# Bias rows written once and read back overlapping, and high parts before low parts within a granule, in a two-layer encoder on one Trainium2 core

## The chip, the cores and the metric

The kernel runs on one core of one Trainium2 chip. The metric is device microseconds for one execution of the whole program, the median of several runs. Times inside a profile are microseconds from the start of the profiled span, unless marked ns.

## The reference, cut to what matters

Input x is 256 tokens by 2048 features, float32. The trunk has two layers. Layer 0: RMSNorm, differential attention with a shared relative-position bias, residual, RMSNorm, squared-ReLU MLP (2048 to 8192 to 2048), residual. Then keys, values and forget gates are computed once from the stream. Layer 1: RMSNorm, queries, forgetting attention over these keys and values, residual, a second MLP, residual, final RMSNorm. The bias, which the change touches, is added to every score of layer 0:

```python
rel = key_pos[None, :] - q_pos[:, None]
bias = jnp.transpose(rel_table[t5_bucket(rel)], (2, 0, 1)).astype(f32)
mask = (key_pos[None, :] // CHUNK) <= (q_pos[:, None] // CHUNK)
s = jnp.where(mask, s + bias[None, :, None], NEG)
```

The bias of a head depends only on key position minus query position, so for each of the 8 heads a row of 383 numbers holds all that is needed.

## The kernel before, in words

Every large product is float32 by three products of shorter numbers: a weight granule is split into a high part (`whi`, a cast on ACT, L180) and a low part (`wlo`, a subtraction on DVE, L183), and the activations are split the same way into the two halves of a 512-column tile, high in columns 0 to 255, low in 256 to 511. High times high, high times low and low times high are added up in PSUM.

A granule is 512 KB of weights. It is loaded into one of four `raw` buffers by SP's queue (`load`, L172), split into one of five `whi` and five `wlo` buffers, and used by one step of PE. A load into a raw buffer waits until the low part of the granule four before has been taken. The main loop (L984) goes through the steps of `order`; at step s it emits the functions registered in `pre[s]`, the split of the granules up to four ahead (three before step 8), `mid[s]`, the low parts and the next loads, the matmuls of the step, and `post[s]`. Instructions of one engine run in that order.

There are two kinds of unit. In a token-major unit ("B", `mm_b`, L185) the activations are the stationary operand: a granule is two blocks of 128 rows by 512 columns, and each needs three matmuls of 512 columns for each of two token halves (L194 to L196), 12 matmuls a step. In a feature-major unit ("A", `mm_a`, L198) the weights are stationary: a granule is four blocks of 128 rows by 256 columns. For each block j and each half n of its columns there is one matmul with the high part over all 512 columns of the activations (`whole`, L209) and one with the low part over the first 256 (`part`, L212), so 8 pairs a step and 4 steps a unit. They alternate, except at k = 15, where `part` comes first. Queries, keys and the MLP's first product are feature-major units.

The bias is prepared early. In `post[5]`, PE multiplies the table by a one-hot matrix (`bias_rows`, L338); the matrix `oh` is an input that the host makes in `bucket_onehot` (L1020). In `pre[6]`, after ACT's sums of squares (`stats0`), `bias_out` copies the 8 rows of 383 numbers to SBUF with DVE (L342) and writes them by SP's queue to a DRAM tile F, each row 128 times (L344). In `pre[8]`, after the evacuation of the first unit and the split of the gate weights (`split_wf`, L967), `bias_in` reads T from F by SP's queue (L352): partition q gets of each head the 256 numbers that begin at 127 - q of the row, by stepping through F with a row length one shorter than it is. POOL then sets the masked quarter of T to a large negative number (L353). The softmax (L414, L415) adds a slice of T to the scores on DVE.

Of the kernel before, what the change touches and what calls it, by code (L numbers as in the profile page):

```python
# [11 lines left out]
F32 = mybir.dt.float32  # L12
# [8 lines left out]
P = 128  # L21
D = 2048
S = 256
HD = 128
FF = 8192
NA = 8
# [3 lines left out]
NEG = -1e30  # L30
# [4 lines left out]
NREL = 383  # L35
# [7 lines left out]
def kernel(ctx: ExitStack, tc: tile.TileContext, *args):  # L43
    (x, rel_table, attn_g, mlp_g, w_qkv, lq1, lk1, lq2, lk2, subln_g, w_o_a, kv_g,
     w_k, w_v, w_f, b_f, w_q, w_o_b, w_in, w_out, fin_g, onehot, out) = args
    nc = tc.nc
# [5 lines left out]
    dr = ctx.enter_context(tc.tile_pool(name="dr", bufs=1, space=DRAM))  # L52
# [29 lines left out]
    h = [sb.tile([P, 2, CW], F32, tag=f"h{c}", name=f"h{c}") for c in range(NCH)]  # L82
# [115 lines left out]
    def mm_a(u, g, k0):  # L198
        bank, xs = u.bank, u.xs()
        hi = g.hi.rearrange("p (k c) -> p k c", k=g.kk)  # L200
        lo = g.lo.rearrange("p (k c) -> p k c", k=g.kk)
        for j in range(g.kk):
            k = k0 + j
            xt = xs[k // 2][:, k % 2, :]
            for n in range(2):
                w = slice(n * P, (n + 1) * P)

                def whole():
                    nc.tensor.matmul(bank[n], hi[:, j, w], xt, start=k == 0, stop=k == 15)  # L209

                def part():
                    nc.tensor.matmul(bank[n][:, 0:S], lo[:, j, w], xt[:, 0:S], start=False, stop=False)  # L212

                if k == 15:
                    part()
                    whole()
                else:
                    whole()
                    part()


    def new_x(tag):
# [111 lines left out]
    bias = {}  # L334
# [5 lines left out]
    def bias_out():  # L340
        bs = sb.tile([NA, 512], F32, tag="e", bufs=2, name="bs")
        nc.vector.tensor_copy(out=bs[:, 0:NREL], in_=bias["p"][0:NA, 0:NREL])  # L342
        F = dr.tile([NA, P, NREL], F32, tag="F", name="F")
        nc.sync.dma_start(out=F, in_=bs[:, 0:NREL].unsqueeze(1).broadcast_to([NA, P, NREL]))  # L344
        bias["F"] = F

    def bias_in():
        T = sb.tile([P, NA, S], F32, tag="tnc", bufs=2, name="T")

        src = bias["F"].rearrange("h q r -> h (q r)")[:, 127:127 + P * (NREL - 1)]  # L350
        src = src.rearrange("h (q r) -> q h r", r=NREL - 1)[:, :, 0:S]
        nc.sync.dma_start(out=T, in_=src)  # L352
        nc.gpsimd.memset(T[0:64, :, 192:256], NEG)  # L353
        bias["T"] = T

    def build_lambda():
# [38 lines left out]
    def diff_head(hd):  # L395
# [13 lines left out]
        def softmax(qt):  # L409
            def run():  # L410
                nk = P * (qt + 1)
                sc = st["sc", qt]
                s = sb.tile([P, 2, S], F32, tag="ssb", bufs=2, name="ssb")
                b = bias["T"][:, hd, S - nk:S].unsqueeze(1).broadcast_to([P, 2, nk])  # L414
                nc.vector.scalar_tensor_tensor(out=s[:, :, 0:nk], in0=sc[:, :, 0:nk], scalar=SCALE, in1=b,  # L415
                                               op0=ALU.mult, op1=ALU.add)
                nm = sb.tile([P, 2], F32, tag="nm", bufs=2, name="nm")
                nc.vector.tensor_reduce(out=nm, in_=s[:, :, 0:nk], op=ALU.max, axis=AX.X, negate=True)
                e = sb.tile([P, 2, S], F32, tag="e", bufs=2, name="e")
                rs = sb.tile([P, 2], F32, tag="rsum", bufs=2, name="rsum")  # L420
                for c in range(2):
                    nc.scalar.activation(out=e[:, c, 0:nk], in_=s[:, c, 0:nk], func=AF.Exp,
                                         bias=nm[:, c:c + 1], accum_out=rs[:, c:c + 1])
                st["e", qt] = e, rs
            return run
# [497 lines left out]
    n, ng = len(order), len(grs)  # L923
# [25 lines left out]
    g = grs[0]  # L949
    split_tiles(g)  # L950
    for k in range(2):
        w = slice(k * CW, (k + 1) * CW)
# [24 lines left out]
    n0.plan(7, lag=2)  # L977
    post[5].append(bias_rows)
    pre[6].append(bias_out)
    pre[8].append(bias_in)  # L980
    pre[12].append(build_lambda)

    ns = LA - 1
    for s in range(n + 2):  # L984
# [13 lines left out]
        if s < n:  # L998
            u, i, ms = order[s]
            if u.bank is None:  # L1000
                if u.apart:
                    u.bank = [ps.tile([P, 512], F32, tag="sc", name="sc") for _ in range(2)]
                else:
                    u.acc = ps.tile([P, 2, 512], F32, tag="acc", name="acc")
                    u.bank = [u.acc[:, m, :] for m in range(2)]
                if u.start is not None:
                    u.start(s)
            g = u.gs[i]
            if u.kind == "B":
                mm_b(u, g, 2 * i, ms)  # L1010
            else:
                mm_a(u, g, 4 * i)
            if i == len(u.gs) - 1:
                u.done(u, s, ms)
# [4 lines left out]

def bucket_onehot():  # L1020

    rel = np.arange(-255, NREL - 255)
    n = np.abs(rel)
    large = 8 + sum((n >= t).astype(np.int64) for t in (12, 16, 23, 32, 46, 64, 91))
    b = np.where(rel > 0, 16, 0) + np.where(n < 8, n, large)
    return (np.arange(32)[:, None] == b[None, :]).astype(np.float32)
# [25 lines left out]
```

## Time and profile before

| | us |
|---|---|
| median of three runs | 2245.37 |
| lowest and highest of the three | 2244.74, 2245.7 |
| the profiled execution | 2244.49 |
| its span in the profile | 2242.7 |

Busy time of an engine is the time in which it ran instructions. Issues of DMAs and waits are not counted as busy. Matmuls are pipelined: the end of one is modelled and overlaps the start of the next, so the pace of PE is read from the distance of starts. PEld is PE's loading of stationary operands, which overlaps its matmuls. The chain of work that ended last is followed back from the last instruction to what released it. In rows, `acc<-x,whi` reads: tile acc is written from tiles x and whi. The granted clock is given as a share of full speed, 1.00 being 2.4 GHz and 0.50 being 1.2 GHz. "SPq" is SP's DMA queue; a row of it covers the issue and, where several issues are merged, the time between them.

### The profile page before, as it was taken

The page shows a single profiled execution, that of the slowest core. Times are in us where ns is not written, and L with a number is a line of the kernel's source. Part 1 is how long each engine was busy: PE and PEld are TensorE (multiplying, and loading weights), DVE is VectorE, ACT ScalarE, POOL GpSimd, SP SyncE. Part 2 cuts the span into 40 slices and gives each one's busy share as a digit, 9 for nine tenths or more (in the row PEclk, how much of TensorE's full clock was granted, in tenths as well). Part 3 has the DMA queues.
Part 4 walks back from the last instruction along what each step waited for, and adds up shares of the span by engine and source line. Part 5 has one row for each costly group of instructions (what it writes and reads, how often), then busy time and mean ns, then how long its engine had stood idle before and what let it go on. Part 6 is the DMA issues. An engine that isn't in the chain of part 4 may idle for free.

```text
span 2242.7 us, 28986 instructions
## 1 busy us (share of the span) xinstructions
PE 2213.4 (99%) x11272; PEld 1877.7 (84%) x11272; DVE 1356.7 (60%) x1768; ACT 1020.8 (46%) x1343; POOL 13.6 (1%) x19
## 2 busy tenths in 40 slices
PE   8799999999999999999999999999999999999998
PEld 6688888888888888888888888888888888888886
DVE  4566666665565566566576566656655655655655
ACT  4455545544344344344554444454434444444443
POOL 0000000000000000000001000000000000000000
PEclk9899999999999999999999999999999999999999
DMA  7665555556656656655556565556566566566564
GB/s 199 199 183 172 166 170 183 173 188 201 183 185 202 195 180 195 192 187 189 177 170 204 173 194 186 180 170 201 183 200 189 185 193 186 188 197 180 187 202 135
DMA packets 319332, 416.06 MB, mean 186 GB/s; under 512 B 15066, under 2 KB 218972, under 8 KB 319068
## 3 DMA queue, kind: packets, MB, share of 16 engines
q1 hardware_dynamic: 319148, 414.20, 58.9%
q8 instruction: 88, 1.44, 0.3%
q14 instruction: 48, 0.39, 0.1%
q10 hardware_dynamic: 48, 0.02, 0.0%
HBM read 410.49 MB, written 3.68 MB: 185 GB/s over the span
## 4 chain that ended last, share of the span: by engine, by line
PE 97%; DMA 2%; DVE 0%; ACT 0%; issue 0%; SPq 0%; DVEq 0%; ACTq 0%
PE acc L209 32%; PE acc L212 16%; PE acc L194 15%; PE acc L196 15%; PE acc L195 15%; DMA raw<-in_w_qkv_a 2%; PE tp L232 1%; PE sc L405 0%; PE sc L748 0%; PE sc L194 0%; PE sc L195 0%; PE sc L196 0%; PE o L806 0%; DMA h<-in_x 0%; PE fp L619 0%; PE o L807 0%
## 5 line engine op out<-in xcount | busy, mean ns | idle before, releaser
L183 DVE TENSOR_TENSOR wlo<-raw,whi 128x1024 fp32r<-128x1024 f32 x767 | 926.1, 1225 | 627.4 <-ACT whi L180 626.8
L180 ACT CAST whi<-raw 128x1024 fp32r<-128x1024 f32 x767 | 795.9, 1048 | 730.5 <-PE acc L196 443.5
L209 PE MATMUL acc<-x,whi 128*128 128x512 f32 x2816 | 996.1, 399 | 17.5 <-ACT whi L180 17.5
L212 PE MATMUL acc<-x,wlo 128*128 128x256 f32 x2816 | 777.7, 281 | 0.5 <-DVE wlo L183 0.5
L209 PEld LDWEIGHTS acc<-x,whi 128*128 128x128 f32 x2816 | 525.7, 188 | 139.6 <-ACT whi L180 17.8
L212 PEld LDWEIGHTS acc<-x,wlo 128*128 128x128 f32 x2816 | 532.9, 189 | 9.2 <-DVE wlo L183 1.0
L194 PE MATMUL acc<-whi,hx 128*128 128x512 f32 x1120 | 436.9, 390 | 0.0
L196 PE MATMUL acc<-whi,hx 128*128 128x512 f32 x1120 | 436.0, 389 | 0.0
L195 PE MATMUL acc<-wlo,hx 128*128 128x512 f32 x1120 | 435.8, 389 | 0.0
L196 PEld LDWEIGHTS acc<-whi,hx 128*128 128x128 f32 x1120 | 210.2, 188 | 43.8
L195 PEld LDWEIGHTS acc<-wlo,hx 128*128 128x128 f32 x1120 | 210.3, 188 | 43.5
L194 PEld LDWEIGHTS acc<-whi,hx 128*128 128x128 f32 x1120 | 210.3, 188 | 43.1
L316 DVE TENSOR_TENSOR zs<-acc,z 128x512 f32<-128x512 f32 x96 | 66.3, 691 | 103.8 <-ACT z L315 103.8
L315 ACT COPY z<-acc 128x512 f32<-128x512 f32 x96 | 56.3, 587 | 157.9 <-PE acc L209 157.9
L590 ACT CAST hx<-s 128x512 fp32r<-128x512 f32 x64 | 39.7, 620 | 143.3 <-DVE s L588 143.3
L194 PE MATMUL acc<-whi,x 128*128 128x512 f32 x256 | 103.4, 404 | 0.0
L195 PE MATMUL acc<-wlo,x 128*128 128x512 f32 x256 | 100.5, 393 | 0.0
L196 PE MATMUL acc<-whi,x 128*128 128x512 f32 x256 | 100.5, 392 | 0.0
L209 PE MATMUL acc<-hx,whi 128*128 128x512 f32 x256 | 91.6, 398 | 0.0
L591 DVE TENSOR_TENSOR hx<-s,hx 128x512 fp32r<-128x512 f32 x64 | 44.3, 692 | 43.9 <-ACT hx L590 43.9
L212 PE MATMUL acc<-hx,wlo 128*128 128x256 f32 x256 | 70.5, 281 | 0.0
L327 DVE TENSOR_TENSOR h<-acc,h 128x512 f32<-128x512 f32 x88 | 56.7, 686 | 14.9 <-PE acc L196 14.9
(172 smaller groups left out, 1169.8 us busy)
## 6 DMA issues: line engine op xcount, KB each, us to landing
raw<-in_w_mlp_in SPq DMA_DIRECT2D x256, 512.0 KB, 4.0
raw<-in_w_mlp_out SPq DMA_DIRECT2D x256, 512.0 KB, 4.2
raw<-in_w_qkv_a SPq DMA_DIRECT2D x96, 512.0 KB, 4.5
raw<-in_w_o_a SPq DMA_DIRECT2D x32, 512.0 KB, 4.3
raw<-in_w_v_b SPq DMA_DIRECT2D x32, 512.0 KB, 3.8
raw<-in_w_k_b SPq DMA_DIRECT2D x32, 512.0 KB, 3.9
raw<-in_w_q_b SPq DMA_DIRECT2D x32, 512.0 KB, 4.2
raw<-in_w_o_b SPq DMA_DIRECT2D x32, 512.0 KB, 3.7
```

What stands on the lines that cost most here:

```text
L180: nc.scalar.copy(out=g.hi, in_=g.raw)
L183: nc.vector.tensor_tensor(out=g.lo, in0=g.raw, in1=g.hi, op=ALU.subtract)
L194: nc.tensor.matmul(bank[m], xh, hi[:, j, :], start=k == 0, stop=False)
L195: nc.tensor.matmul(bank[m], xh, lo[:, j, :], start=False, stop=False)
L196: nc.tensor.matmul(bank[m], xl, hi[:, j, :], start=False, stop=k == nk - 1)
L209: nc.tensor.matmul(bank[n], hi[:, j, w], xt, start=k == 0, stop=k == 15)
L212: nc.tensor.matmul(bank[n][:, 0:S], lo[:, j, w], xt[:, 0:S], start=False, stop=False)
L315: nc.scalar.copy(out=z1, in_=u.acc[:, :, S:2 * S])
L316: nc.vector.tensor_tensor(out=zs, in0=u.acc[:, :, 0:S], in1=z1, op=ALU.add)
L327: nc.vector.tensor_tensor(out=h[c][:, m, :], in0=u.bank[m], in1=h[c][:, m, :], op=ALU.add)
L590: nc.scalar.copy(out=t[:, :, 0:S], in_=s)
L591: nc.vector.tensor_tensor(out=t[:, :, S:2 * S], in0=s, in1=t[:, :, 0:S], op=ALU.subtract)
```

## The change

The host's one-hot matrix is made for relative positions 127 down to -255 instead of -255 up to 127, so that the rows come out reversed. F holds each row once (8 x 383) and is written by ACT's queue. T is read by ACT's queue with a source that overlaps itself: partition q reads, of each head, the 256 numbers that begin at q of the row, so T is reversed along the keys. The mask's memset moves to the first 64 columns and the softmax reads the first nk numbers of T backwards. Apart from this, `mm_a` takes all eight matmuls with the high parts of a granule in a row, then the eight with the low parts; the special order at k = 15 goes.

```diff
-        for j in range(g.kk):
-            k = k0 + j
-            xt = xs[k // 2][:, k % 2, :]
-            for n in range(2):
-                w = slice(n * P, (n + 1) * P)
...
-                if k == 15:
-                    part()
-                    whole()
-                else:
-                    whole()
-                    part()
+        tiles = [(j, n, xs[(k0 + j) // 2][:, (k0 + j) % 2, :], slice(n * P, (n + 1) * P))
+                 for j in range(g.kk) for n in range(2)]
+        for j, n, xt, w in tiles:
+            nc.tensor.matmul(bank[n], hi[:, j, w], xt, start=k0 + j == 0, stop=False)
+        for j, n, xt, w in tiles:
+            nc.tensor.matmul(bank[n][:, 0:S], lo[:, j, w], xt[:, 0:S], start=False, stop=k0 + j == 15)
...
-        F = dr.tile([NA, P, NREL], F32, tag="F", name="F")
-        nc.sync.dma_start(out=F, in_=bs[:, 0:NREL].unsqueeze(1).broadcast_to([NA, P, NREL]))
+        F = dr.tile([NA, NREL], F32, tag="F", name="F")
+        nc.scalar.dma_start(out=F, in_=bs[:, 0:NREL])
...
-        src = bias["F"].rearrange("h q r -> h (q r)")[:, 127:127 + P * (NREL - 1)]
-        src = src.rearrange("h (q r) -> q h r", r=NREL - 1)[:, :, 0:S]
-        nc.sync.dma_start(out=T, in_=src)
-        nc.gpsimd.memset(T[0:64, :, 192:256], NEG)
+        F = bias["F"]
+        src = bass.AP(F.tensor, F.offset, [[1, P], [NREL, NA], [1, S]])
+        nc.scalar.dma_start(out=T, in_=src)
+        nc.gpsimd.memset(T[0:64, :, 0:64], NEG)
...
-                b = bias["T"][:, hd, S - nk:S].unsqueeze(1).broadcast_to([P, 2, nk])
+                b = bias["T"][:, hd, 0:nk][:, ::-1].unsqueeze(1).broadcast_to([P, 2, nk])
...
-    rel = np.arange(-255, NREL - 255)
+    rel = np.arange(127, 127 - NREL, -1)
```

## Rows read from the trace of the kernel before

**Rows 1.** The page: busy time, and the chain's shares by engine.

```profile
PE 2213.4 (99%) x11272; PEld 1877.7 (84%) x11272; DVE 1356.7 (60%) x1768; ACT 1020.8 (46%) x1343; POOL 13.6 (1%) x19
...
PE 97%; DMA 2%; DVE 0%; ACT 0%; issue 0%; SPq 0%; DVEq 0%; ACTq 0%
```

**Rows 2.** The page, groups by line: busy us, mean ns, idle before.

```profile
L209 PE MATMUL acc<-x,whi 128*128 128x512 f32 x2816 | 996.1, 399 | 17.5 <-ACT whi L180 17.5
L212 PEld LDWEIGHTS acc<-x,wlo 128*128 128x128 f32 x2816 | 532.9, 189 | 9.2 <-DVE wlo L183 1.0
L209 PE MATMUL acc<-hx,whi 128*128 128x512 f32 x256 | 91.6, 398 | 0.0
```

**Rows 3.** The chain in order of time, 25 to 80: start, us, what.

```profile
33.25 1.04 ACT whi L180
...
35.57 30.16 DMA raw<-in_w_qkv_a
```

**Rows 4.** Timeline of SP's DMA queue, 25 to 66: start, us, issue.

```profile
29.44 0.82 SPq L344 DMA_DIRECT2D F<-bs  x1
35.57 13.97 SPq L172 DMA_DIRECT2D raw<-in_w_qkv_a  x2
64.38 0.37 SPq L352 DMA_DIRECT2D T<-F  x1
```

**Rows 5.** Windows of 5 us: busy PE, PEld, DVE, ACT, POOL, clock, DMA share, GB/s.

```profile
55.00:60.00 5.00, 0.00 (x0) 0.00 (x0) 0.00 (x0) 0.00 (x0) 0.00 (x0) 0.50 0.47 50
...
65.00:70.00 5.00, 2.62 (x7) 1.93 (x8) 2.69 (x3) 2.09 (x2) 0.16 (x1) 0.50 0.97 317
```

**Rows 6.** Timeline of PE before, around and after the stall: start, us, instruction.

```profile
34.62 0.50 PE L209 MATMUL acc<-x,whi 128*128 128x512 f32 x1
...
49.13 0.28 PE L212 MATMUL acc<-x,wlo 128*128 128x256 f32 x1
66.91 0.80 PE L209 MATMUL acc<-x,whi 128*128 128x512 f32 x1 [17.50 <-ACT whi L180]
...
72.29 0.39 PE L209 MATMUL acc<-x,whi 128*128 128x512 f32 x1
```

**Rows 7.** DMA issues: count, KB each, median us to landing.

```profile
raw<-in_w_qkv_a SPq DMA_DIRECT2D x96, 512.0 KB, 4.5
...
gf<-in_final_norm_g SPq DMA_DIRECT2D x1, 1024.0 KB, 7.0
...
C<-fg_nc SPq DMA_DIRECT2D x1, 16.0 KB, 4.7
```

**Rows 8.** ACT's timeline; T's users: ns min/median/max, first and last start.

```profile
38.71 0.41 ACT L967 CAST wfs<-wf_raw 128x256 fp32r<-128x256 f32 x1
...
L415 DVE SCALAR_TENSOR_TENSOR ssb<-sc,T x16: 415/554/685, 86.2 to 334.8; 128x256 f32<-128x256 f32 x8, 128x512 f32<-128x512 f32 x8
```

**Rows 9.** Timeline of PE within a feature-major unit, around 500 us.

```profile
500.02 0.28 PE L212 MATMUL acc<-x,wlo 128*128 128x256 f32 x1
...
501.08 0.28 PE L212 MATMUL acc<-x,wlo 128*128 128x256 f32 x1
```

**Rows 10.** The same within a token-major unit: a matmul, and its twelfth successor.

```profile
333.60 0.39 PE L194 MATMUL acc<-whi,hx 128*128 128x512 f32 x1
...
336.32 0.39 PE L194 MATMUL acc<-whi,hx 128*128 128x512 f32 x1
```

**Rows 11.** The same at the end of a feature-major unit, 77 to 79.

```profile
77.47 0.40 PE L212 MATMUL acc<-x,wlo 128*128 128x256 f32 x2
77.71 0.40 PE L209 MATMUL acc<-x,whi 128*128 128x512 f32 x1
...
78.07 0.62 PE L209 MATMUL acc<-x,whi 128*128 128x512 f32 x2
78.52 0.28 PE L212 MATMUL acc<-x,wlo 128*128 128x256 f32 x1
```

**Rows 12.** The chain in order of time, 374 to 376: eight transposes.

```profile
374.71 0.87 PE tp L232 x8
```

More of the change, by code (lines that the diff above doesn't have):

```diff
@@ L201, in mm_a @@
         lo = g.lo.rearrange("p (k c) -> p k c", k=g.kk)
-        for j in range(g.kk):
-            k = k0 + j
-            xt = xs[k // 2][:, k % 2, :]
-            for n in range(2):
-                w = slice(n * P, (n + 1) * P)
[L208 to L212, printed above, removed]
-                if k == 15:
-                    part()
-                    whole()
-                else:
-                    whole()
-                    part()
+        tiles = [(j, n, xs[(k0 + j) // 2][:, (k0 + j) % 2, :], slice(n * P, (n + 1) * P))
[4 more added lines that the diff above has]
+            nc.tensor.matmul(bank[n][:, 0:S], lo[:, j, w], xt[:, 0:S], start=False, stop=k0 + j == 15)
     def new_x(tag):
```

## The prediction

> **What bounds the kernel now.** I began with the page's share of busy time and its chain. PE is busy for 2213.4 of 2242.7 us, and the chain that ended last lies 97% on PE and 2% on a DMA [rows 1]. So a step counts only if it shortens what PE does, or a stretch in which PE stands. The groups by line show both: the first matmul line of the feature-major units holds 17.5 us of idle time, put down to ACT's high parts, and these units issue 2816 + 256 = 3072 such matmuls, each with a partner of 256 columns from the low parts [rows 2]. With eight pairs to a granule that is 384 granules.
>
> Next, the stall. The chain in order of time shows one piece of 30.16 us on a raw load that starts at 35.57, and the high part that PE waits for comes after its end [rows 3]. The DMA queue's timeline shows what stood before it: the write of F at 29.44, then two raw loads within 13.97 us, then nothing until the read of T at 64.38 [rows 4]. The windows show why the load crawls: at 55 to 60 us the DMA engines are 0.47 busy but move 50 GB/s, at a granted clock of 0.50; once F is through, 317 GB/s are moved [rows 5]. F is 8 x 128 rows of 383 words, out of eight partitions, 1.5 MB; it keeps about half of the engines occupied at a low rate, and the raw loads share them.
>
> **The change, part by part.**
>
> *The write of F.* It shrinks from 1024 rows of 1532 bytes to 8 of them and moves from SP's queue to ACT's. What goes is the stall. PE's last low part before it starts at 49.13, and 0.12 us later the next matmul would have started, at 49.25. PE starts again at 66.91 at half clock, 1.2 GHz after 2.4 GHz, and has done seven pairs by 72.29 [rows 6]. Seven pairs at the regular pace (0.3533 us, below) take 2.47 us. So the stall with its slow restart costs 72.29 - 49.25 - 2.47 = **20.6 us**. Nothing hides it, since PE is the chain before and after. The low end is 17.5 us, the idle time alone [rows 2]; more than 20.6 can't come out, since PE has no other idle time of this size.
>
> Is something else late instead? The load of 35.57 (the granule at which PE stopped) would land after about 4.5 us, the median of its kind [rows 7], at 40, nine us ahead of 49.25. SP no longer stands at the read of T, so later loads follow each freed buffer. What is new is on ACT. The issue of F stands behind ACT's squares and ahead of the cast at 33.25 [rows 3]; SP's issue of it took 0.82 us [rows 4]. At 4.7 us to landing, as the 16 KB write of C took [rows 7], it lands near 38. ACT comes to the issue of T after the cast of the gate weights, 38.71 to 39.1 [rows 8], so that wait comes out at about nothing. Behind it on ACT stand the high parts of the granules three and four ahead of PE; PE, which began its feature-major granules at 34.62 [rows 6] and takes 2.83 us for each, reaches the first of them after 43, so some 3 us of lateness are covered. T still moves 1 MB. Repeated reads of few bytes have a near row, the final gain's 1 MB in 7.0 us [rows 7], so T lands near 46; it is first used at 86.2 [rows 8], which becomes 65.6. The SBUF end has 128 partitions as before. While T moves, raw loads share the engines, but these moved 317 GB/s beside the same T read [rows 5] and PE needs 512 KB per 2.83 us, 185 GB/s. Cost: nothing, at most 5 us if T's megabyte comes ahead of a load at the rate of that 7.0 us row.
>
> *Reversal.* The one-hot table comes reversed from the host, the DVE add in the softmax reads its bias with step -1, the mask's memset moves to the first 64 columns. DVE is 60% busy [rows 1] and hidden by PE; 16 adds of 0.42 to 0.69 us [rows 8] could double without being seen. Cost nothing.
>
> *The order of matmuls.* The count stays; only neighbours change. Regular pairs: the low part at 500.02 is followed by its third successor at 501.08, so three pairs take 1.06 us, 0.3533 each, a granule 2.827 [rows 9]. In token-major units, where 512 columns follow 512 columns, twelve take 336.32 - 333.60 = 2.72 us, **0.2267** each [rows 10]. So of a pair's 0.3533, 0.1267 are left for the low part, while half of 0.2267 is 0.1133. The difference could belong to the low part (the next weights not ready under so short a matmul), or to the change of size. At a unit's end the code already puts two low parts and two high parts next to each other, and there two low parts take 77.71 - 77.47 = 0.24, **0.12** each, and two high parts 78.52 - 78.07 = 0.45, 0.225 each [rows 11]. Runs of eight short matmuls with weights of their own go at 0.87 / 8 = 0.109 us in the transposes [rows 12], so weight loads don't forbid 0.12.
>
> A changed granule is then 8 x 0.2267 + 8 x 0.12 + 0.007 for the one change of size left (0.1267 - 0.12) = 2.780, which is 0.047 under 2.827; times 384, **17.9 us**, all on PE. The bounds: if the low part's 0.1267 belongs to it wherever it stands, nothing is gained; at 0.1133 a granule is 2.72 and the gain 41 us. At a worse end, each low part takes the 0.189 us that the profile gives a weight load [rows 2]; that is a rival. I take 0.12, the only row with low parts side by side.
>
> The Trainium skill (TensorE: Matmul & The Clock Gate, Back-to-back issue gap) gives a matmul's spacing as its columns over 2.4 GHz plus 2.5 ns, with no term for its neighbour. By that page 512 columns take 0.216 us, an estimate, and the order is worth nothing, which is the first rival. The trace has more, 0.2267 [rows 10], and at the unit's end it does show the neighbour: 0.225 for a high part beside another against the 0.233 that a pair's 0.3533 leaves beside a low part of 0.12 [rows 9, 11].
>
> High parts' buffers come free about a us earlier and low parts are needed two us later. ACT's copy of the second half of a unit's bank may start earlier; ACT and DVE have slack. Nothing is gained there, and nothing lost.
>
> *Sum.* The profiled execution took 2244.49 us, 1.79 of it outside the span. 2244.49 - 20.6 - 17.9 = 2206.0. The median of the runs shown is 0.88 higher, so I give **2207**.
>
> **The rivals.**
>
> *The order is worth nothing.* A low part holds PE for 0.1267 wherever it stands. (The Trainium skill's rule above would have the order not count either.) For it speaks that runs of two could be fed from a weight load already made, which a run of eight can't; against it rows 11 and 12. It gives 2245.4 - 20.6 = 2225. Chance 0.16.
>
> *The low parts run freer still*, at 0.1133: 2245.4 - 20.6 - 41 = 2184. Against it speaks the 0.12 at the unit's end. Chance 0.07.
>
> *The write doesn't get short.* If F's slowness came from its few partitions and not its bytes, ACT would stand at T's issue with the high parts behind it, and PE would stop as before, as much as 20.6 us: 2245.4 - 17.9 = 2228, or anything between. C's write from 16 partitions in 4.7 us speaks against it. Chance 0.06.
>
> *Slower: weight loads in series.* If in a run of eight each low part waits out a whole weight load, 0.189 us, a granule takes 1.813 + 1.512 = 3.325, 0.50 more; times 384 this is 191 us, less the stall's 20.6: 2416. It decides from a low part of 0.1334 us on, where a granule grows by 20.6 / 384 = 0.054. The transposes at 0.109 speak against it, as do loads of 0.188 under token-major matmuls spaced by 0.2267; but nowhere does the trace show eight 256-column matmuls of this type in a row. Chance 0.04.
>
> **How the numbers follow.** The forecast, with its own range 2200 to 2216 (stall 17.5 to 20.6, low part 0.118 to 0.122), has 0.67. The range is 2193 to 2226: it takes in the forecast, the rival without a gain from order and low parts down to about 0.1165, and leaves out the two ends beyond. A measurement of this kernel tells about 0.2% (4.5 us) from no change. Faster by more than that are the first four cases, 0.96 together, of which I give 0.01 to a low part near 0.1334 and so to no change: 0.95, 0.01 and, for the last case, 0.04.
>
> **What would show it.** The windows from 45 to 75 us without idle PE and at a clock of 1.00; no chain piece of 30 us on a raw load; ACT's casts at 39 us not late; the feature-major granule at 2.78 us by the starts, high parts 0.2267 apart and low parts 0.12. The forecast is wrong if PE stops again before 70 us, if a granule still takes 2.83, or if low parts are over 0.13 apart.

## The result and the profile after

The changed kernel takes 2213.56 us (median of four runs, 2213.29 to 2214.53) against 2245.19 for the kernel before: 31.6 us less, a ratio of 0.986 (95% interval 0.9843 to 0.9877). The forecast was 2207 within 2193 to 2226. The sign and the cause of most of it were right; the time came out 6.6 us above the forecast.

The page of the changed kernel: busy time, the chain by engine, the queues. These answer to [rows 1] and, for the line of the high parts, to [rows 2].

```profile
PE 2199.8 (99%) x11272; PEld 1877.9 (85%) x11272; DVE 1354.2 (61%) x1768; ACT 1014.4 (46%) x1343; POOL 13.0 (1%) x19
...
q10 hardware_dynamic: 1104, 1.08, 0.2%
...
PE 99%; DMA 0%; DVE 0%; ACT 0%; issue 0%; SPq 0%; DVEq 0%; ACTq 0%
...
L205 PE MATMUL acc<-x,whi 128*128 128x512 f32 x2816 | 708.2, 393 | 0.0
```

The DMA's 2% of the chain are gone, the line of the high parts (now L205) has no idle time before it, and ACT's queue (q10) carries the megabyte of T. The matmul count is the same. The windows that answer to [rows 5], of the changed kernel:

```profile
45.00:50.00 5.00, 5.00 (x31) 4.42 (x31) 2.27 (x2) 2.58 (x3) 0.52 (x1) 1.00 0.89 280
50.00:55.00 5.00, 5.00 (x31) 4.46 (x30) 4.04 (x9) 2.67 (x4) 0.00 (x0) 1.00 0.67 203
55.00:60.00 5.00, 5.00 (x30) 4.33 (x29) 4.59 (x6) 2.95 (x4) 0.00 (x0) 1.00 0.76 229
60.00:65.00 5.00, 5.00 (x32) 4.48 (x32) 3.33 (x5) 2.24 (x3) 0.00 (x0) 1.00 0.94 306
65.00:70.00 5.00, 5.00 (x30) 4.40 (x29) 4.24 (x8) 2.78 (x9) 0.00 (x0) 1.00 0.63 202
```

PE is busy in every microsecond of these windows, and of the next one to 75, at the full 2.4 GHz. ACT's timeline and the landing of T, of the changed kernel, answer to [rows 4, 8]:

```profile
32.77 0.51 ACTq L332 DMA_DIRECT2D F<-bs  x1
...
38.06 0.40 ACTq L340 DMA_DIRECT2D T<-F  x1
...
39.10 1.05 ACT L180 CAST whi<-raw 128x1024 fp32r<-128x1024 f32 x1
...
T<-F ACTq DMA_DIRECT2D x1, 1024.0 KB, 7.0
```

T is issued 5.3 us after F, between the two halves of the evacuation of the first unit, and the cast behind it starts at 39.10, 0.09 later than the 39.01 before. T takes 7.0 us, as the final gain's row did [rows 7].

The new order, in PE's timeline of the changed kernel (start, us, instruction, count), answers to [rows 9]:

```profile
481.88 2.00 PE L205 MATMUL acc<-x,whi 128*128 128x512 f32 x8
483.72 1.11 PE L207 MATMUL acc<-x,wlo 128*128 128x256 f32 x8
484.67 2.00 PE L205 MATMUL acc<-x,whi 128*128 128x512 f32 x8
```

Eight low parts take 484.67 - 483.72 = 0.95, which is 0.119 each, close to the 0.12 of the forecast. Eight high parts take 1.84, 0.230 each, and not 0.2267. The granule is 2.79, where 2.78 was forecast and 2.827 stood before.

### The profile page after: what moved, and what is told of

Same layout as the page of the kernel before. It is cut to its first block, busy times and chain, and to the rows that moved or that the text cites. A ratio compares the mean times of both kernels' runs of the same rounds, so it can differ in the third digit from the quotient of the medians.

```text
span 2211.9 us, 28985 instructions
## 1 busy us (share of the span) xinstructions
PE 2199.8 (99%) x11272; PEld 1877.9 (85%) x11272; DVE 1354.2 (61%) x1768; ACT 1014.4 (46%) x1343; POOL 13.0 (1%) x19
## 4 chain that ended last, share of the span: by engine, by line
PE 99%; DMA 0%; DVE 0%; ACT 0%; issue 0%; SPq 0%; DVEq 0%; ACTq 0%
PE acc L205 32%; PE acc L207 17%; PE acc L194 15%; PE acc L195 15%; PE acc L196 15%; PE tp L220 1%; PE sc L393 0%; PE sc L736 0%; PE sc L196 0%; PE sc L195 0%; PE sc L194 0%; PE o L794 0%; DMA raw<-in_w_qkv_a 0%; PE fp L607 0%; PE o L795 0%; PE tpo L471 0%
## 5 line engine op out<-in xcount | busy, mean ns | idle before, releaser
L205 PE MATMUL acc<-x,whi 128*128 128x512 f32 x2816 | 708.2, 393 | 0.0
L205 PEld LDWEIGHTS acc<-x,whi 128*128 128x128 f32 x2816 | 508.0, 189 | 92.1
L207 PEld LDWEIGHTS acc<-x,wlo 128*128 128x128 f32 x2816 | 384.1, 190 | 27.6
L207 PE MATMUL acc<-x,wlo 128*128 128x256 f32 x2816 | 392.6, 282 | 0.0
L205 PE MATMUL acc<-hx,whi 128*128 128x512 f32 x256 | 64.9, 395 | 0.0
L196 PEld LDWEIGHTS acc<-whi,x 128*128 128x128 f32 x256 | 48.3, 189 | 10.4
```

Of the source, the lines that this page charges most:

```text
L196: nc.tensor.matmul(bank[m], xl, hi[:, j, :], start=False, stop=k == nk - 1)
L205: nc.tensor.matmul(bank[n], hi[:, j, w], xt, start=k0 + j == 0, stop=False)
```

## Where the time came from

The starts of the first matmul of each stretch of one kind tell the parts from each other. The first feature-major stretch runs from 34.62 to 103.68 before and from 34.72 to 82.92 after, 20.86 less. The same matmuls in an MLP, eight units or 32 granules, in the kernel before and then in the changed one:

```profile
596.75 0.39 PE L209 MATMUL acc<-x,whi 128*128 128x512 f32 x1
...
687.14 0.39 PE L194 MATMUL acc<-whi,hx 128*128 128x512 f32 x1
```

```profile
574.53 0.62 PE L205 MATMUL acc<-x,whi 128*128 128x512 f32 x2
...
663.89 0.40 PE L194 MATMUL acc<-whi,hx 128*128 128x512 f32 x1
```

90.39 became 89.36: 1.03 less, 0.032 for each granule. The eight such stretches, of which two give only 0.94, give 8.1 us. In layer 0 a stretch of 16 granules (202.53 to 250.75 before, 181.60 to 229.65 after) became only 0.17 shorter, in layer 1 about 0.37; these eight stretches of queries and keys give 2.1 us. The token-major stretches behind the first feature-major one are unchanged within about 0.01. So, of the 30.8 us between the spans of the two traces, 20.7 are the stall's and 10.2 the order's.

## The experiments

**Each part alone.** First the bias part with the old order:

```diff
 the bias part as in the change
-        for j, n, xt, w in tiles:
-            nc.tensor.matmul(bank[n], hi[:, j, w], xt, start=k0 + j == 0, stop=False)
...
+                if k == 15:
+                    part()
+                    whole()
+                else:
+                    whole()
+                    part()
```

> The bias part alone, with the old order of matmuls. Theory: the two parts add up, and the first is worth what the traces show at the end of the first feature-major stretch (before 103.68, after 82.92 us, so 20.8, of which 0.2 is the new order): 2245.2 - 20.6 = 2224.6, give or take 1. Rival: the gain is shared (faster steps need earlier loads, or the new order hides a rest of the stall): then over 2 us off, 2222 or 2227.

Measured: 2224.36 us beside 2244.99 for the kernel before, so 20.6 less (ratio 0.9907, 0.9892 to 0.9922). Then the new order with the old bias (the diff is the change's first half):

> The new order alone, with the old bias. Theory: 2245.2 less what the stretches after the first show between the two traces, 10.2 us: 2235.0, give or take 1, with PE standing still from about 49 to 67 us as before. Rival: with all high parts of a granule first, PE stops later or restarts earlier around the stall, and the time is 2 us or more lower, 2233 or less.

Measured: 2234.15 (ratio 0.9951, 0.9936 to 0.9966), 10.8 less. PE stands still for 16.67 us instead of 17.50, so at most 0.9 belongs to the stall and nothing like 2:

```profile
67.12 3.78 PE L205 MATMUL acc<-x,whi 128*128 128x512 f32 x8 [16.67 <-ACT whi L180]
```

The two parts give 31.4 together, the whole change 31.6: they add up.

**Bytes or queue.** The change does two things to F: it is written once, and it goes over ACT's queue. Back on SP's queue, written once:

```diff
-        nc.scalar.dma_start(out=F, in_=bs[:, 0:NREL])
+        nc.sync.dma_start(out=F, in_=bs[:, 0:NREL])
...
-        nc.scalar.dma_start(out=T, in_=src)
+        nc.sync.dma_start(out=T, in_=src)
```

> The change with both bias transfers on SP's queue, F still written once. Theory (the bytes of F on few engines made the stall): SP waits at the read of T only until the small write lands, about 34 us, and the time is that of the changed kernel, 2213.6, give or take 1. Rival (the wait on SP's queue made the stall): PE stands again before 70 us, 2 us or more slower, up to 2224.

Measured: 2214.68 (2213.59 to 2215.66; ratio 0.9864, 0.9847 to 0.988). The trace has no idle PE between 30 and 75 us. From its first feature-major matmul on (36.16 against 34.72 in the changed kernel) no stretch differs by 0.01; what it has more, 1.4 us in this trace, lies before F is even read back. The runs of both overlap, so the queue is worth nothing that can be seen. SP's queue in this run:

```profile
30.99 0.30 SPq L332 DMA_DIRECT2D F<-bs  x1
37.11 4.01 SPq L172 DMA_DIRECT2D raw<-in_w_qkv_a  x2
41.21 0.46 SPq L340 DMA_DIRECT2D T<-F  x1
```

The read follows its loads at once, at 41.21, and not 15 us later as in [rows 4]. Now the other way round, written 128 times on ACT's queue:

```diff
-        F = dr.tile([NA, NREL], F32, tag="F", name="F")
-        nc.scalar.dma_start(out=F, in_=bs[:, 0:NREL])
+        F = dr.tile([NA, P, NREL], F32, tag="F", name="F")
+        nc.scalar.dma_start(out=F, in_=bs[:, 0:NREL].unsqueeze(1).broadcast_to([NA, P, NREL]))
...
-        src = bass.AP(F.tensor, F.offset, [[1, P], [NREL, NA], [1, S]])
+        src = bass.AP(F.tensor, F.offset, [[NREL + 1, P], [P * NREL, NA], [1, S]])
```

> The change with F written 128 times, as before, on ACT's queue, and T read by ACT from it. Theory (bytes): the write still takes some 34 us; ACT stands at the read of T until about 67 us with the high parts behind it, PE stops from about 46 to 68 us and restarts at half clock; 2213.6 + 18 to 28, so 2232 to 2242. Rival (queue): raw loads go on, PE does not stop, 2213 to 2216.

Measured, one run: 2240.51. ACT's timeline, three windows of this run, and the landing of the load that SP issues at about 36.6:

```profile
32.95 1.27 ACTq L332 DMA_DIRECT2D F<-bs  x1
...
67.11 0.40 ACTq L340 DMA_DIRECT2D T<-F  x1
67.54 3.88 ACT L180 CAST whi<-raw 128x1024 fp32r<-128x1024 f32 x4 [27.41 <-DMA F<-bs]
```

```profile
40.00:45.00 5.00, 3.97 (x27) 3.42 (x25) 0.83 (x4) 0.13 (x1) 0.00 (x0) 1.00 0.64 102
45.00:50.00 5.00, 0.00 (x0) 0.00 (x0) 0.00 (x0) 0.00 (x0) 0.00 (x0) 0.84 0.46 50
...
65.00:70.00 5.00, 1.36 (x3) 1.16 (x4) 1.38 (x2) 2.46 (x3) 0.00 (x0) 0.50 0.39 97
```

```profile
raw<-in_w_qkv_a SPq DMA_DIRECT2D x1, 512.0 KB, 23.6
```

The write takes 34 us from its issue on ACT's queue too, ACT stands 27.41 us with the high parts behind it, and PE stops earlier than before, in the window from 40 to 45. This is the wait that the prediction named as a rival, and it is larger than the 20.6 that the rival gave it at most: the first stretch is 26.6 us longer than in the changed kernel. SP's load takes 23.6 us beside the write, although the write is not on SP's queue, and not the 4.5 of its kind [rows 7]. So it is not the order within one queue that slows a load; the DMA engines, which both use, fit. The queue moved without a smaller write thus costs six us more than the old stall, and leaves 4.5 of the order's ten. Bytes and rows of F shrank together, by 128; which of the two sets the 34 us was not tested.

**Why the high parts take 0.230.** First, is it the alternation of the two PSUM banks? Token-major units stay on one for three matmuls.

```diff
-                 for j in range(g.kk) for n in range(2)]
+                 for n in range(2) for j in range(g.kk)]
```

> The change with the runs ordered by bank: the four high parts of the first half of columns, then the four of the second, and the same for low parts. Theory (banks don't matter): no change, 2213 to 2214.5, high parts still 0.234, 0.235, 0.229 ... at the start of a run. Rival (the 0.230 of high parts comes from alternating banks; token-major units stay on a bank for three and take 0.2267): 384 x 0.028 = 10.6 us faster, 2203.

Measured: 2214.48 (2213.49 to 2214.97); the feature-major stretches agree with the changed kernel within 0.01 us. The order of the banks doesn't matter. Then half as many changes of size, with the order turned in every second granule:

```diff
+        for f in ((wholes, parts) if k0 % 8 == 0 else (parts, wholes)):
+            f()
```

> The change with the order turned in every second granule (high, low | low, high), so runs of sixteen and half as many changes of size. Theory (the high parts are slow only in the first few after low parts, 27 ns in all, the first low part 7 ns fast): half of 20 ns saved for each granule, 384 x 0.010 = 3.8 us, 2209 to 2211. Rival (0.230 is what a high part takes in this kind of unit): no change, 2213 to 2214.5.

Measured: 2211.09 (2210.31 to 2211.98; ratio 0.9848, 0.9833 to 0.9863), 2.5 below the changed kernel, with no overlap of their runs, and the lowest median of all runs with every matmul in full. The MLP stretch takes 89.07. PE's timeline of this run, the last row from a window that begins inside a run of sixteen:

```profile
445.83 3.82 PE L207 MATMUL acc<-x,whi 128*128 128x512 f32 x16
449.49 2.08 PE L211 MATMUL acc<-x,wlo 128*128 128x256 f32 x16
451.40 3.82 PE L207 MATMUL acc<-x,whi 128*128 128x512 f32 x16
```

```profile
447.00 2.66 PE L207 MATMUL acc<-x,whi 128*128 128x512 f32 x11
```

The first five high parts take 447.00 - 445.83 = 1.17, 0.234 each; the other eleven 449.49 - 447.00 = 2.49, 0.2264 each, the token-major pace [rows 10]. Sixteen low parts take 1.91, 0.119 each. So 0.230 is no property of the unit: the first five take 1.17 - 5 x 0.2267 = 0.036 more than the settled pace at the resolution of the rows, of which 16 x 0.12 - 1.91 = 0.01 comes back in the low parts. It is lost each time low parts give way to high ones, and after sixteen low parts no more than after eight (the table below). How it goes with shorter runs:

```diff
+        for i in range(0, len(tiles), 2):
+            for j, n, xt, w in tiles[i:i + 2]:
+                nc.tensor.matmul(bank[n], hi[:, j, w], xt, start=k0 + j == 0, stop=False)
+            for j, n, xt, w in tiles[i:i + 2]:
+                nc.tensor.matmul(bank[n][:, 0:S], lo[:, j, w], xt[:, 0:S], start=False, stop=k0 + j == 15)
```

> The change with runs of two: high, high, low, low, instead of eight and eight. Theory (a low part holds PE 0.12 us by its successor's weight load in any order; what is left over depends on how runs fall against each other): from the trace of before at unit ends, 0.2317 + 0.2251 + 0.1192 + 0.1199 = 0.696 for two pairs, a granule 2.784 against 2.7925 in the changed kernel: 384 x 0.009 = 3 us faster, 2210 to 2212. Rival (every change of size costs, so fewer are better): four changes a granule instead of one, between the changed kernel and the old order: 2217 to 2221.

Measured: 2211.57 (2210.84 to 2212.36; ratio 0.985, 0.9835 to 0.9865), 2.0 faster than the changed kernel with four times its changes of size, and where the theory had it. With fours (the same code with 4 in place of 2):

> The change with runs of four high and four low parts. Theory (a fixed cost each time that low parts give way to high ones after a longer run, 20 ns for runs of eight and of sixteen, but 3 ns for runs of two, because less than 27 ns of delay can build up behind two): runs of four between, 8 to 20 ns a change, two changes a granule: 2.789 to 2.813 against 2.7925, 2212 to 2222. Rival (the cost is per granule and falls with the number of changes): 2211.5 to 2213.5.

Measured: 2218.39 (2218.32 to 2218.44; ratio 0.988, 0.9864 to 0.9897), 4.8 slower than the changed kernel, within the theory's range and above the rival's. PE's timelines, runs of two and then runs of four:

```profile
440.35 0.62 PE L206 MATMUL acc<-x,whi 128*128 128x512 f32 x2
440.81 0.40 PE L208 MATMUL acc<-x,wlo 128*128 128x256 f32 x2
441.05 0.63 PE L206 MATMUL acc<-x,whi 128*128 128x512 f32 x2
441.51 0.39 PE L208 MATMUL acc<-x,wlo 128*128 128x256 f32 x2
441.74 0.63 PE L206 MATMUL acc<-x,whi 128*128 128x512 f32 x2
442.21 0.40 PE L208 MATMUL acc<-x,wlo 128*128 128x256 f32 x2
442.44 0.63 PE L206 MATMUL acc<-x,whi 128*128 128x512 f32 x2
```

```profile
440.45 1.09 PE L206 MATMUL acc<-x,whi 128*128 128x512 f32 x4
441.38 0.63 PE L208 MATMUL acc<-x,wlo 128*128 128x256 f32 x4
441.85 1.09 PE L206 MATMUL acc<-x,whi 128*128 128x512 f32 x4
```

With twos, two high and two low parts take (442.44 - 440.35) / 3 = 0.697, a granule 2.79; with fours a granule is twice 1.40, 2.80. The theory behind the twos had this sum right and not its parts: two high parts take 0.463 (0.46, 0.46 and 0.47) and not 0.457, two low parts 0.233 (0.24, 0.23 and 0.23) and not 0.239. The rows have only hundredths; the stretches tell more. If every matmul took its settled pace, 0.2267 and 0.12, a granule would take 2.773. Over that, by the MLP stretch of 32 granules (574.77 to 663.94 with twos, 575.23 to 665.01 with fours, 573.68 to 662.75 with sixteens, each to 0.01):

| run length | stretch, us | granule | over 2.773 | changes | over, each |
|---|---|---|---|---|---|
| 1 (before) | 90.39 | 2.825 | 0.052 | 8 | 0.006 |
| 2 | 89.16 | 2.786 | 0.013 | 4 | 0.003 |
| 4 | 89.79 | 2.806 | 0.033 | 2 | 0.016 |
| 8 (the change) | 89.36 | 2.793 | 0.020 | 1 | 0.020 |
| 16 | 89.07 | 2.783 | 0.010 | 0.5 | 0.020 |

Fewer changes are better from four upwards; below that a change costs less than the long runs suggest, with twos because low parts, at 0.117 each, go below the 0.12 that the sum takes for them.

**What holds a low part at 0.12.** Low parts over 128 columns instead of 256:

```diff
-            nc.tensor.matmul(bank[n][:, 0:S], lo[:, j, w], xt[:, 0:S], start=False, stop=k0 + j == 15)
+            nc.tensor.matmul(bank[n][:, 0:P], lo[:, j, w], xt[:, 0:P], start=False, stop=k0 + j == 15)
```

> The change with low-part matmuls over 128 columns of the activations instead of 256; the low product of the second token half is left out. Theory (a low part's 0.12 us is its successor's weight load, not its own columns): low parts stay 0.11 to 0.12 apart and the time is within 8 us below the changed kernel, 2205 to 2214. Rival (columns set it): 0.057 to 0.065 apart, 384 x 8 x 0.055 = 170 us faster, 2045.

Measured, one run: 2194.86, 10 below the range that the theory gave. PE's timeline of this run, the last two rows from windows that begin inside a run:

```profile
440.93 2.07 PE L205 MATMUL acc<-x,whi 128*128 128x512 f32 x8
442.83 1.01 PE L207 MATMUL acc<-x,wlo 128*128 128x128 f32 x8
443.67 2.07 PE L205 MATMUL acc<-x,whi 128*128 128x512 f32 x8
```

```profile
442.89 0.95 PE L207 MATMUL acc<-x,wlo 128*128 128x128 f32 x7
...
443.95 1.78 PE L205 MATMUL acc<-x,whi 128*128 128x512 f32 x7
```

With half the columns the eight take 0.84 instead of 0.95, and the eight high parts behind them 1.90 instead of 1.84. Inside the run they differ. The first low part takes 442.89 - 442.83 = 0.06, as the rival would have all of them; the other seven take (443.67 - 442.89) / 7 = 0.111 each, and the first high part behind them 443.95 - 443.67 = 0.28. So the columns set only the first, and something that does not shrink with them holds the others at 0.111. That the transposes go at 0.109 [rows 12] shows little, since their operands are plain float32 and not the type of the split parts (fp32r in ACT's rows). A weight load would fit, as every matmul has one of its own, but the run shows only the floor, not what makes it. The 0.12 with 256 columns is a little above this floor and above half a high part, 0.1133, so neither alone sets it.

**The old exception at the end of a unit.** The old order, without it:

```diff
         for j, n, xt, w in tiles:
             nc.tensor.matmul(bank[n], hi[:, j, w], xt, start=k0 + j == 0, stop=False)
-        for j, n, xt, w in tiles:
             nc.tensor.matmul(bank[n][:, 0:S], lo[:, j, w], xt[:, 0:S], start=False, stop=k0 + j == 15)
```

> The change with the old alternation of high and low part, but without the old exception at k = 15. Theory (alternating pairs hold one of two rhythms, three pairs in 1.04 or in 1.06 us, set by how the stretch is entered, and 1.04 is what loads of 0.12 and columns of 0.2267 give): MLP stretches stay in one rhythm from end to end: either 90.4 to 90.5 us (1.06; total 2224 to 2226) or 88.7 to 88.9 (1.04; total 2206 to 2209). Rival (an alternation costs its 6.6 ns each time, layer 0 being quicker for another reason, such as its tiles): 1.06 everywhere but in layer 0, 2224 to 2226, with layer 0 again at 1.04 in about half of its pairs.

Measured: 2225.48 (2224.94 to 2227.58; ratio 0.9914, 0.9899 to 0.9929). The MLP stretch takes 90.44 (577.05 to 667.49). Both sides had this time in their range, so the run does not tell them apart. That there are two rhythms is seen in the kernel before, in layer 0, in a timeline to be set beside [rows 9]:

```profile
218.08 0.39 PE L209 MATMUL acc<-x,whi 128*128 128x512 f32 x1
218.31 0.28 PE L212 MATMUL acc<-x,wlo 128*128 128x256 f32 x1
...
219.12 0.39 PE L209 MATMUL acc<-x,whi 128*128 128x512 f32 x1
```

Three alternating pairs in 1.04 us here, 0.3467 each, 1.06 there. 0.3467 is the sum of 0.2267 and 0.12: by it the quick rhythm loses nothing. What puts a stretch into one or the other stays open.

## Why the prediction was right or wrong

*The stall* was forecast at 20.6 us. The first stretch gives 20.7 without the order's share, the bias part alone 20.6. The idle time and the slow restart at half clock both went, and nothing came in their place. The write did get short: T's issue waits for it (in the run with 128 copies on ACT the wait is 27.41 us), and here T is issued 5.3 us behind F. F's rows still come from eight partitions, so these alone were not what made it slow. The Trainium skill (DMA: Bandwidth & Descriptors, Rules for kernel authors) says that a DMA whose outermost dimension has fewer than 16 entries runs on at most that many engines; F's write has 8 outermost, and the trace agrees: 0.47 of the 16 engines are busy in the stall [rows 5], just under half. The same page (Issuing engines are not separate DMA queues) says that another issuing engine gives no bandwidth of its own, and the two queue experiments agree: 2214.68 with the small write on SP, 2240.51 with the large one on ACT. The prediction gave the queue no price of its own, and none was seen.

*T's read and ACT's wait* were forecast to cost nothing: T lands at 45, first use is at 63.9, and ACT's casts come 0.09 us later. *Reversal*: the DVE adds took 415 to 685 ns before and 411 to 684 after, so nothing.

*The order* was forecast at 17.9 us and gave 10.2 in the trace and 10.8 alone. Two terms were mis-sized. The first is the step "a changed granule is 8 x 0.2267 + 8 x 0.12 + 0.007". The low part was right. The high part was taken from token-major rows at 0.2267, and a high part in a run of eight takes 0.230, because the first five after low parts are slow; the change of size costs 0.020 and not 0.007. That is 2.793 instead of 2.780, and the 256 MLP granules gave 8.1 us where 0.047 would have given 12.0. The second is "times 384", with 0.3533 for every pair of before. In layer 0 a good part of the pairs already ran at 0.3467, and some in layer 1, so their granules had less to lose: 2.1 us from 128 granules where 0.047 would have given 6.0. Rows 9 came from one stretch, and rows from layer 0 would have shown it. The time lies within the forecast's own 2200 to 2216, but by luck in part: the slow end of that range stood for a stall of 17.5 or a low part of 0.122, and neither came.

*The rivals.* The order is not worth nothing, as the formula for the spacing of matmuls in the Trainium skill (TensorE: Matmul & The Clock Gate, Back-to-back issue gap), which has no neighbour in it, would have had it; runs of one and of sixteen are 13 us apart (2224.36 and 2211.09) with the same matmuls. The prediction took that formula too far: the section gives it for an isolated matmul, and says that in a stream of weight loads and matmuls both set the spacing. Of the gain that the forecast took from the order, something over half came. Low parts at 0.1133 throughout did not come, and weight loads in series, at 0.189, are out.

## What to carry to other kernels

A transfer that repeats rows for the reader's convenience holds the DMA engines that it uses until all copies are through, here for 34 us, and loads that share these engines wait with it, here 30 us instead of 4.5; write once and let the read overlap. Moving a transfer to another queue without making it smaller can move the wait to a worse place, here to the engine that feeds PE. And before a pace is multiplied by a count, it should be read in more than one stage: the same pairs ran at two paces here, and neighbours changed the pace of a long matmul from 0.2267 to 0.234.

## What was not expected of the hardware

An alternation of 512- and 256-column matmuls with weights of their own can hold either of two rhythms for a whole unit, 1.04 or 1.06 us for three pairs, at the same granted clock of 1.00. After sixteen short matmuls, the first five long ones take 0.234 each before they come back to 0.2267. A change of size costs 0.016 to 0.020 us behind four or more short matmuls, and 0.003 to 0.006 behind one or two. In a run of short matmuls over 128 columns only the first comes at the 0.06 that the columns suggest, the others 0.111 apart. Runs of two and of sixteen come out within half a microsecond of each other (2211.57 and 2211.09), with runs of four 7 us above. In runs of two it is the low parts that make up for slow high parts, at 0.117 instead of 0.12; why they can was not found.
